# Branch outputs kept as parts, own PSUM tiles, sums on one engine, moved modulation blocks: a change to a two-layer diffusion backbone

## The chip, the core and the metric

One core of a Trainium2 chip runs the whole program. The metric is device time in microseconds (us) from launch to end, the median over executions; lower is better. Engines: TensorE (PE, with its weight loads as PEld), VectorE (DVE), ScalarE (ACT), GpSimd (POOL) and SyncE (SP). DMAs are issued here mostly by SP (loads) and by ACT (stores to scratch in DRAM).

## The reference

Two layers over 512 latent tokens and 256 context tokens of width 1024. Both layers read the context; only the first has to produce it, so layer 0 works on 768 tokens and layer 1 on 512. All is fp32.

```
sh1, sc1, g1, sh2, sc2, g2 = split(silu(c) @ w_mod[l] + b_mod[l], 6)   # per stream
h = adaLN(x, sh1, sc1)
f, nq, nk, nv, cq, ckv, kr, g = split(h @ w_in)
y_f   = real(fft2(f))                     # branch A, 4 channel groups
y_na  = neighbourhood attention(nq, nk, nv) + context keys    # branch B
y_mla = latent attention(cq, ckv, kr)     # branch C
gate  = sigmoid(g)                        # 3 x 1024 per token
mix   = sum_b(gate_b * (y_b @ w_branch_b)) @ w_out
x = LayerNorm(alpha * x + (1 + g1) * mix)
h = adaLN(x, sh2, sc2)
x = LayerNorm(alpha * x + (1 + g2) * ((silu(h @ w_gate) * (h @ w_up)) @ w_down))
```

The modulation vectors (sh1 ... g2) are 12 blocks of 512 columns per layer: blocks 0 and 1 are sh1, 2 and 3 sc1, 4 and 5 g1, 6 and 7 sh2, 8 and 9 sc2, 10 and 11 g2.

## The kernel before, in words

**Precision.** Every large fp32 product is made of three fp32r products: each operand x is kept as a high part (a rounded copy, made by ACT) and a low part (x minus the high part, made by DVE or POOL), and hi x hi, lo x hi and hi x lo are added in PSUM. Activations stand in the big tiles AH and AL; weights are cut the same way as they arrive (whi by ACT at L210, wlo by DVE or POOL at L211).

**Stages of a layer.** Fourier (branch A); NA (branch B, one step per head pair and block of queries); MLA (branch C); gates, whose results are stored in DRAM (gbuf); merge; the out-projection with its LayerNorm (`out_norm`); FFN; the FFN's own out-projection.

**Order.** A step is a Python closure; a list of steps is emitted in program order, and the tile framework then orders each engine's instructions by a timing model of its own. Where steps are `pinned`, PE's order is that of the list. `weave` spreads a list of fill steps between main steps by their costs. PSUM has 8 banks, each held by one tile of `self.ps()`; a bank is written again only after its readers are done. A tile with `bufs` n rotates over n buffers: the next writer of a buffer waits for the last reader, a store included.

**The branch outputs.** Each branch ends in fp32 tiles `ys` (128 channels x tokens), four per branch and layer, which ACT's queue stores to `ybuf[b]` in DRAM (L993 Fourier, L1237 NA, L1543 MLA). In the merge, `y_load(b)` reads branch b back: four times a load from SP into `yr`, a cast to `yh` by ACT (L1630) and a difference `yl` by DVE (L1631).

**The merge.** 24 units (b, j): branch b times output chunk j of 128 channels. `proj` does 4 x 3 matmuls per token range against `w_br` (L1680), then DVE forms (gate + 1) x product from the gate tile `th` and PSUM (L1683) and adds it to `m[j]` (L1686; POOL for branch 1, DVE for branch 2). `th_load` brings the gate tiles two units ahead. `y_load(1)` and `y_load(2)` are issued after unit j = 3 of the branch before; `y_load(0)` in the gates. From unit 4 on, the residual xr is scaled by halves beside it (L1736, POOL, and L1728 for its vectors, DVE). After all units, `split` makes AH and AL of m (ACT L1706, DVE L1707).

**Gates and FFN in seven products.** Gates and FFN work two output chunks at a time by a seven-product scheme (`seven`, matmuls L509). It needs sums and differences of the halves of the activations: `sums` forms whole tiles t = AH + AL (`whole`, L434), differences (`less`, L438), and parts tp of them (`parts`: ACT cast L443, difference L444). There are four such places, the gates and the FFN of each layer. `whole` is done four times and `parts` three times per place, each over 4 chunks; two of the former and two of the latter are on POOL, the rest on DVE.

**The FFN's start.** The hidden chunks 0 and 1 (layer 1: and 2) are done directly, by `unit(f, part)`: g multiplies with `w_gate` and passes SiLU by ACT to `hx` (L1922), u multiplies with `w_up` and DVE multiplies both (L1935). `early` are the units on the first half of the tokens, which run between the transposes (`t0`, `t1`) of the last token blocks out of the LayerNorm; `late` those on the second half. In layer 0, `unit(1, full)` runs over all 768 tokens beside the sums: its context range uses one PSUM tile for both g and u (`s["c", f]`, 2 x 256 columns).

**Modulation blocks.** `mod_fill` makes for each block a step with 32 matmuls (L532) from four 512 KB tiles `mraw` of w_mod, and a finishing step: transposes (L554) and a reduction, or for the gate blocks 4, 5, 10 and 11 one product per half (L544) and a store. Layer 0's first four blocks are done at the start. Its others and layer 1's blocks in MOD_NA are fill in layer 0's NA (12 blocks); layer 1's remaining eight are fill in layer 0's gates.

## Time and profile before

| | |
|---|---|
| median of 3 runs | 2390.05 us (2388.05 to 2396.88) |
| profiled execution, its span | 2387.02 us, 2385.2 us |
| mean granted PE clock | 0.982 |
| busy PE, DVE, ACT, POOL | 95%, 56%, 46%, 42% |
| HBM read, written | 262.06 MB, 47.48 MB |

A line of the profile is named by its line number in the kernel (L1631) and by its tiles, out<-in. Instructions in one row may be several of a kind in a row (x4), the time is then that of all. "[5.56 <-DVE yl L1631]" behind an instruction says that its engine stood idle for 5.56 us before it, and what ended that. The granted clock is PE's, 1.00 being full speed.

### The profile page before, as it was taken

What the parts mean: (1) busy time and instruction counts of PE and PEld (TensorE: products, weight loads), DVE (VectorE), ACT (ScalarE), POOL (GpSimd) and SP (SyncE); (2) the same over time, 40 slices, a digit from 0 to 9 for tenths busy, and PEclk for the clock granted to TensorE, in tenths of its full rate; (3) what the DMA queues carried; (4) which work ended last, traced back from release to release, by engine and by line L of the source; (5) the groups of instructions that cost most, each with busy time, mean ns of one, the idle gap of its engine ahead of it and who ended that gap; (6) DMA issues with size and microseconds to landing.
All of it is one profiled execution on the core that took longest, in us unless ns stands there. A gap on an engine that the chain in (4) does not pass through costs nothing. (4 is left out here: it accounts for less than half of the span.)

```text
span 2385.2 us, 36359 instructions
## 1 busy us (share of the span) xinstructions
PE 2272.1 (95%) x13794; PEld 1971.4 (83%) x13794; DVE 1331.3 (56%) x2339; ACT 1101.7 (46%) x2432; POOL 992.4 (42%) x755
## 2 busy tenths in 40 slices
PE   6999999999999998999999999999999998999997
PEld 4877678878987878999988888787878877999875
DVE  7334456667544568555541462344668458788634
ACT  4335567644432254444442352575765425545532
POOL 2411143124248356334449353324413676323483
PEclk9999999999999999999999999999999999999998
DMA  9436521117674331222262243222214643323432
GB/s 340 145 138 235 187 78 62 54 56 281 225 252 158 115 120 58 98 98 97 71 227 75 80 149 105 79 69 91 87 68 168 207 150 107 113 94 105 142 115 62
DMA packets 105403, 307.71 MB, mean 129 GB/s; under 512 B 12070, under 2 KB 21228, under 8 KB 105228
## 3 DMA queue, kind: packets, MB, share of 16 engines
q1 hardware_dynamic: 86444, 261.48, 32.4%
q10 hardware_dynamic: 15552, 38.63, 4.2%
q0 software_dynamic: 3232, 5.28, 0.8%
q8 instruction: 108, 1.77, 0.3%
q14 instruction: 67, 0.55, 0.1%
HBM read 262.06 MB, written 47.48 MB: 130 GB/s over the span
## 5 line engine op out<-in xcount | busy, mean ns | idle before, releaser
L211 POOL TENSOR_TENSOR wlo<-raw,whi 128x512 fp32r<-128x512 f32 (+2 forms) x420 | 564.4, 1352 | 879.5 <-ACT whi L210 841.6
L210 ACT CAST whi<-raw 128x512 fp32r<-128x512 f32 (+1 forms) x447 | 273.2, 616 | 426.8 <-PE ps L1680 85.7
L509 PE MATMUL ps<-tp,whi 128*128 128x384 f32 (+1 forms) x1120 | 276.0, 316 | 4.9 <-ACT p L481 3.0
L509 PEld LDWEIGHTS ps<-tp,whi 128*128 128x128 f32 x1120 | 196.1, 189 | 9.5 <-ACT p L481 3.4
L509 PE MATMUL ps<-AH,whi 128*128 128x384 f32 (+1 forms) x636 | 199.3, 316 | 4.2 <-DVE hx L490 1.9
L509 PE MATMUL ps<-AH,wlo 128*128 128x384 f32 (+1 forms) x636 | 198.6, 313 | 1.2 <-DVE wlo L211 1.2
L277 PE MATMUL ps<-AH,whi 128*128 128x512 f32 (+1 forms) x584 | 188.4, 367 | 9.8 <-ACT hx L1922 7.4
L509 PE MATMUL ps<-AL,whi 128*128 128x384 f32 (+1 forms) x636 | 197.2, 312 | 0.0
L277 PE MATMUL ps<-AL,whi 128*128 128x512 f32 (+1 forms) x584 | 183.0, 360 | 1.5 <-DVE AL L733 1.5
L277 PE MATMUL ps<-AH,wlo 128*128 128x512 f32 (+1 forms) x584 | 183.5, 360 | 0.0
L509 PE MATMUL ps<-tp,wlo 128*128 128x384 f32 (+1 forms) x560 | 176.4, 315 | 0.4 <-DVE wlo L211 0.4
L2035 PE MATMUL ps<-whi,hx 128*128 128x512 f32 x520 | 164.5, 397 | 8.3 <-ACT hx L2027 4.9
L325 PE MATMUL ps<-whi,AH 128*128 128x512 f32 (+1 forms) x352 | 132.7, 385 | 2.9 <-DVE th L1683 2.9
L325 PE MATMUL ps<-whi,AL 128*128 128x512 f32 (+1 forms) x352 | 134.9, 384 | 0.0
L325 PE MATMUL ps<-wlo,AH 128*128 128x512 f32 (+1 forms) x352 | 134.4, 382 | 0.0
L277 PEld LDWEIGHTS ps<-AH,whi 128*128 128x128 f32 x584 | 101.7, 193 | 34.1 <-ACT hx L1922 7.8
L509 PEld LDWEIGHTS ps<-AH,whi 128*128 128x128 f32 x636 | 120.2, 189 | 7.4 <-DVE hx L490 2.6
L2035 PEld LDWEIGHTS ps<-whi,hx 128*128 128x128 f32 x520 | 99.3, 191 | 31.2 <-ACT hx L2027 5.5
L509 PEld LDWEIGHTS ps<-AH,wlo 128*128 128x128 f32 x636 | 120.3, 189 | 1.8 <-DVE wlo L211 1.6
L509 PEld LDWEIGHTS ps<-AL,whi 128*128 128x128 f32 x636 | 120.0, 189 | 0.8 <-issue 0.8
L277 PEld LDWEIGHTS ps<-AL,whi 128*128 128x128 f32 x584 | 100.0, 191 | 19.7 <-DVE AL L733 2.4
L1736 POOL TENSOR_TENSOR xr<-xr,gb 128x512 f32<-128x512 f32 x80 | 114.5, 1447 | 0.4
(340 smaller groups left out, 5671.1 us busy)
## 6 DMA issues: line engine op xcount, KB each, us to landing
mraw<-in_w_mod_dram SPq DMA_DIRECT2D x80, 512.0 KB
raw<-in_w_down_dram SPq DMA_DIRECT2D x44, 512.0 KB
raw<-in_w_g_dram SPq DMA_DIRECT2D x40, 512.0 KB
raw<-in_w_gate_dram SPq DMA_DIRECT2D x36, 512.0 KB
raw<-in_w_up_dram SPq DMA_DIRECT2D x26, 512.0 KB
raw<-in_w_br_dram SPq DMA_DIRECT2D x24, 512.0 KB
gb<-th ACTq DMA_DIRECT2D x24, 384.0 KB
th<-gb SPq DMA_DIRECT2D x24, 384.0 KB
```

The source lines that it names most:

```text
L210: hi_eng(hi[:, :n], x)
L211: lo_eng.tensor_sub(lo[:, :n], x, hi[:, :n].bitcast(F32))
L277: self.nc.tensor.matmul(ps, w.at(wt, ws), at[:, k0 + kc, cols], start=kc == 0 and i == 0, stop=kc == nk - 1 and i == 2)
L325: self.nc.tensor.matmul(ps, a[:, k0 + kc, tok], w.at(b, ws), start=kc == 0 and i == 0, stop=kc == 2 * nb - 1 and i == 2)
L509: nc.tensor.matmul(ps, ws[0].at(wt, w), act[at], start=new and kc == 0 and i == 0, stop=kc == 3 and i == 2, skip_group_check=True)
L1736: i = op(x[:, c], x[:, c], self.gbt[g][:, c])
L2035: nc.tensor.matmul(ps, h[a][:, tok], w.at(b, ws), start=f == seq[0] and i == 0, stop=f == NF - 1 and i == 2)
```

## The change

Six edits:

- `y_store` replaces the store of a branch output. ACT casts the high part into a tile of its own, DVE subtracts it in place, and ACT's queue stores both parts into two DRAM buffers per branch. Fourier uses one new tile `yh`, NA one of half the tokens, twice per head pair, MLA the tile `qrh` of its queries. `y_load` then is eight loads, no cast and no difference, into four buffers for each part, in two pools in turn; it is issued at the units k = 1 and k = 9.
- g and u of `unit` take a PSUM tile for each range, the context too.
- `sums` has `whole` and `parts` on DVE alone.
- Layer 1's blocks 10 and 11 leave layer 0's NA and go between the early FFN units of layer 1; its blocks 8 and 9 leave layer 0's gates and go between the early FFN units of layer 0. Their first four tiles are loaded right ahead of `out_norm`.
- The split of m into AH and AL is emitted per chunk, in the units of branch 2.
- Some tiles of NA in layer 1 have 512 columns instead of 768.

```diff
@@ -48,7 +48,8 @@
 PB = 1
 PB = 1
 LO_POOL = ((0, 3, 5), (3,))
-MOD_NA = (4, 5, 10, 11)
+MOD_NA = (4, 5)
+MOD_FFN = ((8, 9), (10, 11))
 THP = 2
 MADD_POOL = (True, False)
 PIPE_C = 8
@@ -446,16 +447,16 @@
         def first(ws):
             x, y, z = (self.t("tt", [P, 4, half], f"t{i}") for i in range(3))
             whole(y, 0, e, nc.vector)
-            whole(x, 0, d, nc.gpsimd)
-            whole(z, 4, d, nc.gpsimd)
+            whole(x, 0, d, nc.vector)
+            whole(z, 4, d, nc.vector)
             less(y, x, y)
             less(x, z, x)
             less(z, z, y)
             parts(2, z, nc.vector)
-            parts(3, x, nc.gpsimd)
+            parts(3, x, nc.vector)
             whole(x, 4, e, nc.vector)
             less(x, x, z)
-            parts(4, x, nc.gpsimd)
+            parts(4, x, nc.vector)
             s["t1"] = y
 
         def second(ws):
@@ -602,7 +603,7 @@
         self.A = lambda: (self.AH, self.AL)
         self.mod = [cp.tile([P, 48, 2], F32, name=f"mod{l}") for l in range(DEPTH)]
         self.gvec = [[self.dr.tile([2, D], F32, name=f"gvec{l}{w}") for w in range(2)] for l in range(DEPTH)]
-        self.ybuf = [self.dr.tile([512, T], F32, name=f"yb{b}") for b in range(3)]
+        self.ybuf = [[self.dr.tile([512, T], F32, name=f"yb{b}{i}") for i in range(2)] for b in range(3)]
         self.zbuf = [self.dr.tile([NT, P, D], F32, name=f"zb{l}") for l in range(DEPTH)]
         self.bias = [self.dr.tile([P, H, 2, 256], F32, name=f"bd{l}") for l in range(DEPTH)]
         self.vt1 = cp.tile([P, NV1], F32, name="vt1")
@@ -790,6 +791,19 @@
 
         return [fn(ty, h) for h in range(0, H, BH) for ty in range(2)]
 
+    def y_store(self, b, c, ys, hi, tt, n=1):
+
+
+        nc = self.nc
+        rows = slice(c * P, (c + 1) * P)
+        for i in range(n):
+            cols = slice(i * tt // n, (i + 1) * tt // n)
+            h = hi()[:, :tt // n]
+            nc.scalar.copy(h, ys[:, cols])
+            nc.vector.tensor_sub(ys[:, cols].bitcast(F32R), ys[:, cols], h.bitcast(F32))
+            nc.scalar.dma_start(self.ybuf[b][0][rows, cols], h.bitcast(F32))
+        nc.scalar.dma_start(self.ybuf[b][1][rows, :tt], ys[:, :tt])
+
 
     def fourier_open(self, l):
 
@@ -990,7 +1004,7 @@
                         nc.vector.tensor_add(ys[:, 640:768], rev1(pa), rev1(bs))
                     if s == (1 if cx else 0):
                         tt = T if cx else NLAT
-                        nc.scalar.dma_start(self.ybuf[0][g * P:(g + 1) * P, :tt], ys[:, :tt])
+                        self.y_store(0, g, ys, lambda: self.t("fz", [P, T], "yh", F32R, 1), tt)
                 return f
             return [Step(fn(s), [], (2.7, 0.7)[s]) for s in range(2 if cx else 1)]
 
@@ -1061,7 +1075,7 @@
         halves = [(slice(0, 64), slice(64, 128)), (slice(64, 128), slice(0, 64))]
 
         def ev_q(parts):
-            qs = [self.t(pool, [P, T], f"qs{j}", F32R) for j in range(2)]
+            qs = [self.t(pool, [P, T if cx else NLAT], f"qs{j}", F32R) for j in range(2)]
             for j in range(2):
                 h0, h1 = halves[j]
                 for ps, cols in parts:
@@ -1158,7 +1172,7 @@
                 for j in range(2):
                     nc.gpsimd.tensor_add(bt[:, j], bt[:, j], self.mask)
                 self.bt = bt
-                self.nys = self.t("na", [P, T], "ys", F32, 1)
+                self.nys = self.t("na", [P, tt], "ys", F32, 1)
             kh, kl = self.kk[hp]
             st["ys"], st["p"] = self.nys, []
             if i % 2 == 0:
@@ -1234,7 +1248,7 @@
                                          tile_position=(0, 64 * j), skip_group_check=True)
             nc.vector.tensor_mul(st["ys"][:, (i - 1) * P:(i + 1) * P], y[:, :2 * P], sh["w"])
             if i == (NT if cx else NTL) - 1:
-                nc.scalar.dma_start(self.ybuf[1][hp * P:(hp + 1) * P, :tt], st["ys"][:, :tt])
+                self.y_store(1, hp, st["ys"], lambda: self.t("na", [P, T // 2], "yh", F32R, 1), tt, 2)
 
         f = 1.0 if lat else 0.5
         return dict(scores=scores, norm=norm, transpose=transpose, values=values, c=(0.9 * f, 0.9 * f, 2.0 * f * u))
@@ -1540,7 +1554,7 @@
                                      tile_position=(0, 64 * j))
             nc.vector.tensor_mul(st["ys"][:, (i - 1) * P:(i + 1) * P], y[:, :2 * P], sh["w"])
             if i == nq - 1:
-                nc.scalar.dma_start(self.ybuf[2][hp * P:(hp + 1) * P, :tt], st["ys"][:, :tt])
+                self.y_store(2, hp, st["ys"], lambda: self.t("m3", [P, T], "qrh", F32, 1).bitcast(F32R), tt)
 
         f = 1.0 if lat else 0.33
         return dict(scores=scores, norm=norm, transpose=transpose, values=values, c=(1.95 * f, 1.3 * f, 2.9 * f * u))
@@ -1613,7 +1627,7 @@
         s = {"y": {}}
         fill = []
         if l == 0:
-            fill = self.mod_fill([(1, nb) for nb in range(12) if nb not in MOD_NA], 5)
+            fill = self.mod_fill([(1, nb) for nb in range(12) if nb not in MOD_NA + MOD_FFN[0] + MOD_FFN[1]], 5)
             st += self.bias_steps(1)
         left = 3 * KC - self.ahead[l]
 
@@ -1621,14 +1635,10 @@
             def fn(ws):
                 yh, yl = [], []
                 for c in range(4):
-                    r = self.t("my", [P, tt], "yr", F32, 2)
-                    nc.sync.dma_start(r, self.ybuf[b][c * P:(c + 1) * P, :tt])
-                    i = (4 * b + c) % 7
-                    pool, n = ("my", 4) if i < 4 else ("mg", 3)
-                    yh.append(self.t(pool, [P, tt], "yh", F32R, n))
-                    yl.append(self.t(pool, [P, tt], "yl", F32R, n))
-                    nc.scalar.copy(yh[c], r)
-                    nc.vector.tensor_sub(yl[c], r, yh[c].bitcast(F32))
+                    pool = ("my", "mg")[b % 2]
+                    for i, (x, tag) in enumerate(((yh, "yh"), (yl, "yl"))):
+                        x.append(self.t(pool, [P, tt], tag, F32R, 4))
+                        nc.sync.dma_start(x[c].bitcast(F32), self.ybuf[b][i][c * P:(c + 1) * P, :tt])
                 s["y"][b] = (yh, yl)
             return Step(fn)
 
@@ -1684,6 +1694,10 @@
                                                    ALU.add, ALU.mult)
                 if b > 0:
                     (nc.gpsimd if MADD_POOL[b - 1] else nc.vector).tensor_add(m, m, th)
+                if b == 2:
+                    nc.scalar.activation(self.AH[:, j, :tt], m, AF.Copy, scale=0.5)
+                    nc.vector.scalar_tensor_tensor(self.AL[:, j, :tt], m, 0.5, self.AH[:, j, :tt].bitcast(F32),
+                                                   ALU.mult, ALU.subtract)
             return [Step(fn, [(io["w_br"][l, b, j // 2], 1024, "w")] if j % 2 == 0 else [], 3.9 if cx else 2.6)]
 
 
@@ -1693,7 +1707,7 @@
             if k + 2 < len(units):
                 main += [th_load(k + 2)]
             main += proj(b, j)
-            if j == 3 and b < 2:
+            if k in (1, KC + 1):
                 main += [y_load(b + 1)]
             if k == 0:
                 main += [self.open("xr", "left"), self.open("gb", "left"), Step(lambda ws: self.load_xr(l, nt))]
@@ -1701,14 +1715,10 @@
                 main += [Step(lambda ws, i=k - SCALE_AT: self.scale_xr(i // 2, True, (i % 2,)))]
         st += [Step(m_open)] + main
 
-        def split(ws):
-            for j in range(KC):
-                nc.scalar.activation(self.AH[:, j, :tt], s["m"][j], AF.Copy, scale=0.5)
-                nc.vector.scalar_tensor_tensor(self.AL[:, j, :tt], s["m"][j], 0.5,
-                                               self.AH[:, j, :tt].bitcast(F32), ALU.mult, ALU.subtract)
-
-        st += [Step(split), self.close("gb", "mg", "my")]
-        st += [self.open("ln", "left"), Step(lambda ws: self.ln_open(l, 0, cx))]
+        st += [self.close("gb", "mg", "my")]
+        st += [self.open("ln", "left"), Step(lambda ws: self.ln_open(l, 0, cx)), self.open("mod", "left")]
+        begin, *self.mods = self.mod_fill([(1, nb) for nb in MOD_FFN[l]], 4)
+        st += [begin]
         self.out_norm(l, 0, [[(io["w_out"][l, nh, b], 1024, "w") for b in range(4)] for nh in range(2)], self.A, None, 3)
 
     def load_xr(self, l, nt):
@@ -1909,12 +1919,8 @@
                 if ws:
                     s["g", f] = ws[0]
                 pr = []
-                s["c", f] = self.ps() if CTX in part else None
                 for c in part:
-                    if c == CTX:
-                        pr.append((s["c", f][:, :NCTX], c))
-                    else:
-                        pr.append((self.ps()[:, :c.stop - c.start], c))
+                    pr.append((self.ps()[:, :c.stop - c.start], c))
                 block(s["g", f], pr)
                 if ("sg", f) not in s:
                     s["sg", f] = self.t("fx", [P, tt], "hx", F32, 4)
@@ -1926,10 +1932,7 @@
                     s["u", f] = ws[0]
                 pr = []
                 for c in part:
-                    if c == CTX:
-                        pr.append((s["c", f][:, NCTX:], c))
-                    else:
-                        pr.append((self.ps()[:, :c.stop - c.start], c))
+                    pr.append((self.ps()[:, :c.stop - c.start], c))
                 block(s["u", f], pr)
                 for ps, cols in pr:
                     nc.vector.tensor_mul(h_tile(f)[:, cols], s["sg", f][:, cols], ps)
@@ -1979,8 +1982,9 @@
         late = [Step(unit(f, [d])[k], [], c) for f, k in parts]
         t0, t1 = self.tail_tr
         tp, t_sums, t_first = self.sums(tt // 2)
-        st += pinned(early[:1] + [t0] + early[1:2] + [t1] + early[2:] + late)
-        st += [self.close("ln", "xr"), self.open("ft", "right"), self.open("tt", "right"), t_sums]
+        m0, m1 = self.mods[:2], self.mods[2:]
+        st += pinned(m0[:1] + early[:1] + [t0] + m0[1:] + early[1:2] + [t1] + m1[:1] + early[2:] + m1[1:] + late)
+        st += [self.close("mod", "ln", "xr"), self.open("ft", "right"), self.open("tt", "right"), t_sums]
         g, u = unit(1, full)
         rg, ru = reqs(1)
         if cx:
```

## Rows read from the trace of the kernel before

**Rows 1.** The page's first part: busy us of each engine, share of the span, instructions.

```profile
PE 2272.1 (95%) x13794; PEld 1971.4 (83%) x13794; DVE 1331.3 (56%) x2339; ACT 1101.7 (46%) x2432; POOL 992.4 (42%) x755
```

**Rows 2.** Waits of PE: line, what released it; us in total, times, longest.

```profile
PE ps L277 <- ACT hx L1922: 7.4, 1, 7.4
...
PE ps L1680 <- DVE yl L1631: 5.6, 1, 5.6
...
PE ps L1680 <- DVE m L1683: 3.1, 1, 3.1
```

**Rows 3.** Windows around gaps: us, busy (PE, PEld, DVE, ACT, POOL), PEclk, DMA share, GB/s.

```profile
703.50:710.53 7.03, 3.89 (x23) 3.11 (x22) 6.48 (x6) 2.44 (x4) 6.52 (x4) 1.00 0.86 328
710.53:714.10 3.57, 3.57 (x9) 2.88 (x10) 3.57 (x8) 0.83 (x1) 3.57 (x4) 0.52 0.83 251
...
772.66:778.90 6.24, 6.24 (x19) 5.38 (x20) 4.60 (x6) 1.46 (x2) 5.29 (x3) 0.51 0.26 84
879.40:890.72 11.32, 7.10 (x46) 6.51 (x45) 10.21 (x20) 7.61 (x17) 7.92 (x6) 1.00 0.56 189
890.72:894.95 4.23, 4.23 (x15) 4.23 (x16) 4.23 (x4) 0.47 (x1) 4.13 (x3) 0.60 0.00 0
...
922.37:925.70 3.33, 3.33 (x16) 3.33 (x17) 0.51 (x2) 1.28 (x3) 3.33 (x3) 0.51 0.00 0
...
1988.56:2007.85 19.29, 13.26 (x106) 12.45 (x105) 18.04 (x31) 11.56 (x26) 15.07 (x8) 1.00 0.39 136
2021.84:2035.57 13.73, 8.47 (x48) 6.58 (x46) 13.26 (x27) 8.92 (x20) 10.18 (x6) 0.85 0.35 116
2035.57:2038.40 2.83, 2.83 (x13) 2.83 (x14) 0.97 (x2) 0.00 (x0) 2.35 (x2) 0.51 0.51 178
```

**Rows 4.** Timeline of ACT, FFN of layer 0: start, us, instruction, idle before.

```profile
921.04 0.51 ACT L443 CAST tp<-t 128x384 fp32r<-128x384 f32 x1 [1.63 <-DVE t L438]
```

**Rows 5.** Timeline of DVE, then of POOL, in the merge of layer 0.

```profile
705.90 3.98 DVE L1631 TENSOR_TENSOR yl<-yr,yh 128x768 fp32r<-128x768 f32 x2
...
760.59 12.02 DVE L1631 TENSOR_TENSOR yl<-yr,yh 128x768 fp32r<-128x768 f32 x1 [0.62 <-ACT yh L1630]
...
777.17 1.05 DVE L1707 SCALAR_TENSOR_TENSOR AL<-m,AH 128x768 fp32r<-128x768 f32 x1 [0.91 <-ACT AH L1706]
...
766.33 1.81 POOL L1686 TENSOR_TENSOR m<-m,th 128x768 f32<-128x768 f32 x1
768.10 2.48 POOL L1736 TENSOR_TENSOR xr<-xr,gb 128x512 f32<-128x512 f32 x2
```

**Rows 6.** Instructions by line: ns min/median/max, first and last start us.

```profile
L1631 DVE TENSOR_TENSOR yl<-yr,yh x24: 678/973/12018, 558.3 to 1914.0; 128x768 fp32r<-128x768 f32 x12, 128x512 fp32r<-128x512 f32 x12
...
L1630 ACT CAST yh<-yr x24: 614/725/847, 550.6 to 1913.3; 128x768 fp32r<-128x768 f32 x12, 128x512 fp32r<-128x512 f32 x12
...
L444 POOL TENSOR_TENSOR tp<-t,tp x32: 740/1310/5956, 536.7 to 2035.5; 128x384 fp32r<-128x384 f32 x16, 128x256 fp32r<-128x256 f32 x16
L444 DVE TENSOR_TENSOR tp<-t,tp x16: 411/549/1379, 535.1 to 2026.4; 128x384 fp32r<-128x384 f32 x8, 128x256 fp32r<-128x256 f32 x8
```

**Rows 7.** Timeline of POOL, FFN of layer 1.

```profile
2026.63 10.06 POOL L444 TENSOR_TENSOR tp<-t,tp 128x256 fp32r<-128x256 f32 x4 [2.75 <-ACT tp L443]
```

**Rows 8.** Timeline of PE: one mod block, its two finishes.

```profile
171.17 1.02 PE L544 MATMUL ps<-modsb,sel 128*2 128x512 f32 x2
...
677.36 1.93 PE L532 MATMUL ps<-mraw,sT 128*32 128x256 f32 x32
...
687.76 0.60 PE L554 MATMUL ps<-ident,modsb 128*128 128x128 f32 x4
```

**Rows 9.** Window over branch B (NA) of layer 0, columns as in rows 3.

```profile
150.00:347.00 197.00, 191.64 (x1454) 146.22 (x1453) 93.16 (x257) 106.22 (x328) 45.48 (x39) 0.98 0.47 164
```

**Rows 10.** Timeline of ACT, then of DVE, in the gates of layer 1.

```profile
1863.78 0.33 ACTq L1592 DMA_DIRECT2D gb<-th  x1
...
1868.45 0.42 DVE L487 TENSOR_TENSOR th<-ps,p 128x256 f32<-128x256 f32 x1 [4.89 <-DMA gb<-th]
```

## The prediction

> **What bounds the kernel now.** I read the page first: TensorE (PE) is busy 2272.1 of 2385.2 us, 95%, and no other engine passes 56% [rows 1]. The kernel is matmul-bound, so time is won only where PE stands still, and where it runs slowly afterwards: the clock row of the page (not needed here) is full nearly everywhere, so the places to look for are single gaps. The list of PE's waits names them: 7.4 us once for the SiLU tile hx of the FFN's first blocks, 5.6 us once for yl, the low part of a branch output, 3.1 us once for the first gated sum m [rows 2]. Then I cut windows around each gap, to see the idle time and the granted clock behind it. After every one of these gaps the clock stands at 0.51 to 0.60 of full, the lower of its two levels (1.2 against 2.4 GHz), for 3.3 to 6.2 us [rows 3]. So a gap costs its length and, behind it, the stretch at half clock times (1 minus the clock). Both are in my sum; the second part is where PE is "busy" and yet loses.
>
> **The change part by part.** Gains are negative, in us of the profiled execution.
>
> *A, own PSUM tiles for gate and up of the first FFN blocks (layer 0).* Before, the context columns of gate and up share one PSUM bank, so up's context matmuls wait until ScalarE (ACT) has read gate's. That read, hx, is queued on ACT behind the casts of the sums, each of which waits for VectorE (DVE): the cast just ahead of it started at 921.04 after 1.63 us of waiting [rows 4]. PE waited 7.4 us [rows 2], then ran 3.33 us at clock 0.51 [rows 3]: 7.4 + 3.33 x 0.49 = 9.0. With its own bank up needs nothing of hx. Behind it come products that need the sums' parts, which may not be ready. If they were ready no sooner than hx was, only the context block itself would be won: 24 matmuls, of which 16 took 3.33 us at 0.51, so 24 x 3.33 / 16 x 0.51 = 2.5. Ends -2.5 and -9.0; I take **-8.0**, since the sums' parts are spread over that stretch and only a last one should be late.
>
> *B, the split of branch outputs leaves the merge: branch 2 in layer 0.* One DVE difference (L1631) took 12.02 us, against a median of 0.97 for this line, while GpSimd (POOL) ran back to back beside it [rows 5, 6]. PE stood 5.6 us [rows 2] and then ran 6.24 us at 0.51: 5.6 + 6.24 x 0.49 = 8.7. After the change these parts come from DRAM ready-made; the line is gone. What could be late next is another DVE instruction with two SBUF inputs that falls into the same crowded stretch: the split of m (L1707), which the change emits here chunk by chunk; but the scheduler had put it at 777.17, right behind, already [rows 5], so the per-chunk edit by itself I cost at 0. Ends 0 and -8.7, I take **-8.0**.
>
> *C, the same at the merge's start in layer 0.* DVE finishes scaling at about 705.9, then does two such differences, 3.98 us, and only then the sum m that PE waits for [rows 5]. The wait is 3.1 us [rows 2], the clock costs 3.57 x 0.48 = 1.7: 4.8. But the DMA engines are 0.86 busy there at 328 GB/s [rows 3], and the change reads each branch output as two parts: 8 loads of 384 KB instead of 4, for branch 1 issued at unit 1 where PE stands here. I leave 1.4 to the DMA and take **-3.4** (ends 0 and -4.8).
>
> *D, sums on VectorE alone.* At each of the four places 16 two-input operations (8 sums L434, 8 differences L444) move from POOL to DVE. POOL's L444 has a median of 1.31 us and a longest of 5.96, DVE's 0.55 [rows 6]; DVE gets 16 x 0.55 = 8.8 us more work per place. In the FFN of layer 1 PE is busy 8.47 of 13.73 us, 5.3 idle, while POOL takes 10.06 us for four L444 [rows 3, 7]; the clock at 0.85 over that window and 0.51 behind it costs 13.73 x 0.15 + 2.83 x 0.49 = 3.4, of which the first part also counts idle time, so some 2.6: 7.9 in all. DVE is 13.26 of 13.73 busy there, so its 16 operations at the shortest 0.41 [rows 6] add up to 6.6 us of DVE time against POOL's 10.06: part of the wait stays. I take **-6.0** (ends +3 and -7.9). The other three places have no such gap on PE: 0.
>
> *E, mod blocks moved into the FFN's starts.* A block is 32 matmuls, 1.93 us, and a finish of 0.60 (transposes, blocks 8 and 9) or 1.02 (blocks 10 and 11) [rows 8]. The four come to 2 x (1.93 + 0.60) + 2 x (1.93 + 1.02) = 10.96 us of PE, taken out of the attention of layer 0, where PE is busy 191.64 of 197 [rows 9], and out of a gate stretch without idle time: there they are nearly all gain. They go between the first FFN blocks, where PE idles 11.32 - 7.10 = 4.2 us (layer 0) and 19.29 - 13.26 = 6.0 (layer 1), with 4.23 x 0.40 = 1.7 of clock behind the first [rows 3]: 11.9 us of room for 10.96 of work. Their order is pinned, so not every block meets a hole; those that miss move without gain. The 2 MB of mod weights are issued on SP (SyncE's queue) ahead of w_out's loads, where DMA has room. I take **-7.0**, ends 0 and -11.0.
>
> *F, the split at the branches.* What the merge loses, 12 casts and 12 differences per layer (0.73 and 0.97 us at the median) [rows 6], the branches gain, on engines half idle there (ACT 106.22 of 197, DVE 93.16) [rows 9]. New is a wait: the tile of the high part is single (one in the Fourier stage, one of half width in NA, a borrowed query tile in MLA), so the next copy into it waits on ACT until the store has landed. The trace of before has no such store, the nearest is the gates' tile: stored by ACT at 1863.78, and DVE could write it again at 1868.45 after 4.89 us of idling [rows 10], some 4.7 us from issue. Behind the waiting copy, ACT's exponentials and casts of the next head pair are queued, and PE waits for those. In NA the two halves follow each other directly, 8 stores a run; in MLA 8 more. Ends: 0 (the scheduler puts other ACT work between, or PE has enough ahead) and 16 x 4.7 = 75. I take **+4**, near the lower end, because ACT has half its time free and the instruction order is planned around a wait that the planner knows of.
>
> Smaller tiles for layer 1 cost and give nothing that these rows show: 0.
>
> Sum: -8.0 - 8.0 - 3.4 - 6.0 - 7.0 + 4 = -28.4. The profiled execution took 2387.0 (its span is 2385.2); 2387.0 - 28.4 = 2358.6. It lay 3.0 under the median of the runs, 2390.05, so the forecast is 2361.6.
>
> **The rivals.**
> *R1, slower: ACT is held at the stores.* For: ACT runs in order, two copies in NA meet the same half tile at once, and landing took 4.7 us [rows 10]. Against: ACT half idle, PE's waits in NA are 5.4 us in 197 now [rows 9]. Price: at 3 us of PE for each of 16 stores, 48 in place of 4: 2406. It decides from 2.0 us a store on: (2390 - 2357.6) / 16.
> *R2, the merge becomes a matter of DMA.* Each branch now brings 3.1 MB in one burst, 9 us at 328 GB/s, in stretches already 0.86 full [rows 3]; gates' and weights' loads stand behind it on SP. B and C (11.4) are lost and half of E: 2361.6 + 11.4 + 3.5 = 2376.5. Against: the burst is issued seven units, over 25 us, before its use.
> *R3, DVE and POOL slow each other.* The 12.02 us beside a busy POOL [rows 5] shows that a DVE difference can take twelve times its length, and POOL still has its weight splits. Then the sums, now all on DVE, are no faster: D's 6.0 and 5.5 of A go, and the sums of the two out-projections' gates lose 1.5 each: 2361.6 + 14.5 = 2376. The Trainium skill ("GPSIMD Engine Reference", section "1. Specifications") says that GpSimd shares its SBUF interfaces with VectorE, in contention with DVE instructions with two SBUF inputs, and these sums are such; the 12.02 us row agrees with it. By that rule the other way out is also open: less POOL work is less contention, which is my -6.0.
> *R4, the gaps move.* The order on each engine is planned anew for the whole kernel; new gaps of the old size elsewhere give 2388. For: the gaps of before stand although a planner laid out the order. Against: A and B are single, named causes, which are removed.
>
> **How the numbers follow.** Forecast 0.52 (by itself 2350 to 2371), R1 0.13, R2 0.10, R3 0.12, R4 0.13. What a measurement can tell from no change is 0.5%, 12 us: faster is below 2378, slower above 2402. Faster: 0.52 and three quarters of R2 and R3, 0.17, together 0.69. Slower: R1 without its milder part, 0.11. The rest, 0.20, is the same. The upper ends together, 9.0 + 8.7 + 4.8 + 7.9 + 11.0 = 41.4 with F at 0, give 2349; I set the low end at 2346, and the high end at 2392, past R4, so that R1 is what is left out.
>
> **What the changed profile would show.** A: no wait of PE for hx, ctx matmuls of up directly behind the latent ones. B, C: L1631 gone, no half clock in branch 2 of layer 0's merge; the y loads finished before unit 8 and 16. D: four L444 of layer 1's FFN in a row on DVE at 0.4 us. E: mod matmuls between the transposes of the FFN's start, fewer idle us there, and attention of layer 0 shorter by 5 to 6. F: ACT idle ahead of the copies in y_store, released by DMA; if these idle times exceed 2 us and PE's waits in NA and MLA grow with them, it is R1 and I am wrong. I am also wrong if PE's idle total hardly falls while all the named gaps are gone.

## The result and the profile after

The changed kernel took 2367.48 us (median of 4 runs, 2355.63 to 2371.37) against 2389.05 us for the kernel before (4 runs): a ratio of 0.9904, 95% interval 0.9886 to 0.9921. It is faster by about 1%, 21.6 us; 28.4 were forecast. Its profiled execution took 2369.68 us.

The page's first part and the main waits of PE in the changed kernel (line numbers are higher by 1 to 15 after the edits; columns as in [rows 1, 2]):

```profile
PE 2264.3 (96%) x13794; PEld 1965.7 (83%) x13794; DVE 1292.1 (55%) x2411; ACT 1106.2 (47%) x2440; POOL 934.1 (39%) x691
```

```profile
PE ps L326 <- ACT AH L1698: 6.9, 1, 6.9
PE ps L278 <- POOL wlo L212: 5.1, 1, 5.1
...
PE ps L510 <- ACT p L482: 4.2, 4, 2.4
...
PE ps L533 <- DMA mraw<-in_w_mod_dram: 2.7, 1, 2.7
```

The three named waits of [rows 2] are gone (hx, yl, m), but others stand here: for the split of m (AH) at the end of layer 1's merge, for a weight difference (wlo) on POOL in layer 1's FFN start, for mod weights in layer 0's gates, and for copies p. The last are not new in sum (4.5 us in four waits before), but 3.4 of the 4.2 us are now in layer 0's FFN, where there were none. PE works the same 13794 matmuls in 7.8 us less than in [rows 1], at a mean granted clock of 0.985 for 0.982, and idles 9.5 us less (2385.2 - 2272.1 = 113.1 before, 2367.9 - 2264.3 = 103.6 after), where the three waits alone were 16.1. One more thing is odd at first sight: DVE does 72 more instructions in 39 us less. Some 14 us of that come with the sums alone (1317.3 us busy in that kernel, below); the merges do 33 us less (65.80 to 41.01 and 37.39 to 29.44 below), and part of that is done in the branches now.

Windows over the two merges, changed kernel, layer 0 and layer 1 (columns as in [rows 3]):

```profile
683.20:788.00 104.80, 104.80 (x602) 92.46 (x602) 41.01 (x64) 22.84 (x34) 86.15 (x58) 1.00 0.70 253
1846.60:1924.80 78.20, 71.31 (x319) 58.99 (x318) 29.44 (x34) 19.20 (x33) 61.45 (x49) 0.96 0.72 253
```

and the same stretches in the kernel before:

```profile
688.10:805.20 117.10, 108.40 (x592) 94.16 (x591) 65.80 (x77) 28.82 (x42) 81.64 (x57) 0.96 0.58 199
1868.80:1942.90 74.10, 71.20 (x319) 58.90 (x318) 37.39 (x44) 24.48 (x43) 68.68 (x49) 0.98 0.64 209
```

Layer 0's merge has no idle PE left and is 12.3 us shorter; layer 1's is 4.1 longer, with 6.9 us of idle PE. That idle time stands in its last part, where the DMA share is 0.24:

```profile
1890.00:1915.00 25.00, 18.11 (x79) 14.67 (x78) 12.03 (x6) 4.38 (x7) 23.05 (x19) 0.92 0.24 75
```

In the 40 us ahead of it, shown below under the spread loads, the share is 0.95 and PE is never idle.

To see where time went, I cut each trace at the first matmul of a stage, or at the last of the one before. The table gives the lengths before, and the difference for the changed kernel and for four kernels that have one part of it each. They are single executions, so differences under about 2 us say nothing alone.

| stage (layer) | before, us | changed | parts | PSUM | sums | mods |
|---|---|---|---|---|---|---|
| start | 158.2 | +1.2 | -0.2 | -0.3 | +1.5 | +0.6 |
| NA (0) | 195.7 | -7.4 | -0.9 | -0.8 | -1.1 | -8.0 |
| MLA (0) | 179.6 | +1.3 | +1.3 | +0.1 | -0.5 | +1.2 |
| gates (0) | 154.6 | 0.0 | +2.0 | +0.1 | +1.4 | -3.9 |
| merge (0) | 117.1 | -12.3 | -13.1 | -8.3 | +0.5 | -1.6 |
| out_norm, FFN start (0) | 95.7 | +1.3 | +1.7 | 0.0 | -1.5 | +1.3 |
| FFN (0) | 318.4 | -3.6 | +1.3 | +4.7 | -5.5 | +1.1 |
| down (0), Fourier (1) | 300.4 | 0.0 | -0.1 | -0.1 | -1.7 | +0.2 |
| NA, MLA (1) | 282.3 | +0.2 | +2.3 | +0.3 | -1.8 | +0.4 |
| gates (1) | 66.8 | -2.9 | +0.5 | -0.2 | -2.3 | -0.1 |
| merge (1) | 74.1 | +4.1 | +5.1 | +0.1 | +0.2 | -4.1 |
| out_norm, FFN start (1) | 71.6 | +2.1 | +0.3 | +1.5 | +0.5 | +8.5 |
| FFN, down (1) | 353.7 | -1.8 | -1.0 | -1.3 | -8.2 | +1.3 |
| sum | 2368.2 | -17.8 | -0.8 | -4.2 | -18.5 | -3.1 |

The PSUM kernel's profiled execution was its second fastest of 12 (2382.86, median 2392.57), so its column flatters it; that of the mods kernel was its slowest (2383.89, median 2381.91).

One entry teaches more than the rest: the PSUM kernel gains 8.3 us in layer 0's merge, which its edit doesn't touch. The wait for yl isn't there. The DVE difference that took 12.02 us in [rows 5] stands at the same place, beside the same kinds of POOL operations, but is short:

```profile
759.46 1.34 DVE L1631 TENSOR_TENSOR yl<-yr,yh 128x768 fp32r<-128x768 f32 x1 [0.62 <-ACT yh L1630]
```

In the other kernels that keep this difference it took 12.05 to 12.37 us. So the long hold can be absent in a kernel that does the same work here, and a gain of 8 us in this merge doesn't need stored parts.

### The profile page after: what moved, and what is told of

Its sections match the earlier page's. It is cut to its first block, busy times and chain, and to the rows that moved or that the text cites. A ratio compares the mean times of both kernels' runs of the same rounds, so it can differ in the third digit from the quotient of the medians.

```text
span 2367.9 us, 36388 instructions
## 1 busy us (share of the span) xinstructions
PE 2264.3 (96%) x13794; PEld 1965.7 (83%) x13794; DVE 1292.1 (55%) x2411; ACT 1106.2 (47%) x2440; POOL 934.1 (39%) x691
## 5 line engine op out<-in xcount | busy, mean ns | idle before, releaser
L212 POOL TENSOR_TENSOR wlo<-raw,whi 128x512 fp32r<-128x512 f32 (+2 forms) x420 | 588.1, 1410 | 928.2 <-ACT whi L211 876.9
L510 PEld LDWEIGHTS ps<-AH,wlo 128*128 128x128 f32 x636 | 120.5, 189 | 1.0 <-POOL wlo L212 0.6
L278 PEld LDWEIGHTS ps<-AH,wlo 128*128 128x128 f32 x584 | 100.3, 193 | 21.5 <-POOL wlo L212 5.4
```

The source lines that it names most:

```text
L212: lo_eng.tensor_sub(lo[:, :n], x, hi[:, :n].bitcast(F32))
L278: self.nc.tensor.matmul(ps, w.at(wt, ws), at[:, k0 + kc, cols], start=kc == 0 and i == 0, stop=kc == nk - 1 and i == 2)
L510: nc.tensor.matmul(ps, ws[0].at(wt, w), act[at], start=new and kc == 0 and i == 0, stop=kc == 3 and i == 2, skip_group_check=True)
```

## The experiments

Four kernels: before, with one part of the change each.

**Stored parts alone.** `y_store` and `y_load` (with its new places k = 1 and 9), and the smaller tiles.

```diff
-                nc.scalar.dma_start(self.ybuf[1][hp * P:(hp + 1) * P, :tt], st["ys"][:, :tt])
+                self.y_store(1, hp, st["ys"], lambda: self.t("na", [P, T // 2], "yh", F32R, 1), tt, 2)
...
-                    yh.append(self.t(pool, [P, tt], "yh", F32R, n))
+                        nc.sync.dma_start(x[c].bitcast(F32), self.ybuf[b][i][c * P:(c + 1) * P, :tt])
```

> The kernel before with y_store and y_load alone. My theory: it carries the whole gain in layer 0's merge, both waits (yl, m) and the half clock behind them gone, that merge 12 us shorter, and costs 1 to 3 us in NA and MLA: 8 to 11 us faster than before. Rival R1 (ACT held at the stores): NA and MLA together more than 10 us longer, no gain. On the new wait of PE for mod weights at the start of layer 0's gates (2.7 us idle, 3.4 us of clock in the changed kernel): if the eight y loads ahead of them on SP cause it, it is here; if a slow weight split on POOL beside the sums causes it, it is not here. On the 6.9 us wait for AH at the end of layer 1's merge: if the split of m per chunk causes it, it is not here; if the new loads do, it is.

Measured: ratio 0.9995 (0.9983 to 1.0008), 2387.78 us: nothing. Layer 0's merge is 13.1 us shorter, and all of it is paid back elsewhere. Hardly by ACT: the copies of `y_store` in the changed kernel waited for DVE only, never for a store.

```profile
L802 ACT CAST yh<-ys x24: 389/512/837, 81.3 to 1631.8; 128x384 fp32r<-128x384 f32 x8, 128x256 fp32r<-128x256 f32 x8, 128x768 fp32r<-128x768 f32 x4, 128x512 fp32r<-128x512 f32 x4
...
L802 ACT CAST qrh<-ys x8: 622/740/855, 418.9 to 1783.2; 128x768 fp32r<-128x768 f32 x4, 128x512 fp32r<-128x512 f32 x4
...
  DVE ys L998: 10.9, 4
  DVE ys L1249: 8.0, 3
  DVE ys L1555: 4.9, 2
  DVE ys L1004: 2.9, 4
```

(The lines below the two are what ended ACT's idle time ahead of them: four kinds, all DVE.) One other copy did wait for a store: MLA's own cast into the borrowed tile qrh, twice, 1.8 us in all (1.8 with stored parts alone too). The longer of the two, with the store issued ahead of it:

```profile
1712.59 0.33 ACTq L804 DMA_DIRECT2D yb<-qrh  x1
...
1714.65 0.61 ACT L1449 CAST qrh<-qr 32x512 fp32r<-32x512 f32 x1 [1.60 <-DMA yb<-qrh]
```

The hold on DVE is not gone from layer 0's merge either. In the stretch where the branch's difference took 12 us, the addition to m now takes as long, here with stored parts alone:

```profile
765.69 11.04 DVE L1695 TENSOR_TENSOR m<-m,th 128x768 f32<-128x768 f32 x1
```

Without the sums it is 10.59 us, in the changed kernel nothing is held there. But PE is busy for all of this merge in each of these kernels (104.00 of 104.00 us here), so this addition, unlike yl, had time to spare. The edit took away the instruction for which PE waited, and not the hold.

NA and MLA are 2.7 us longer in both layers together (-0.9, +1.3 and +2.3), within the 1 to 3 that were expected and far from R1's 10. So R1 is out. The largest payback is layer 1's merge, +5.1, where PE waits 5.3 us for AH; the split per chunk is not in this kernel, so it is not needed for that wait. No wait for mod weights is here, so the eight loads alone do not make it.

**Own PSUM tiles alone.**

```diff
-                s["c", f] = self.ps() if CTX in part else None
                 for c in part:
-                    if c == CTX:
-                        pr.append((s["c", f][:, :NCTX], c))
-                    else:
-                        pr.append((self.ps()[:, :c.stop - c.start], c))
+                    pr.append((self.ps()[:, :c.stop - c.start], c))
```

> The kernel before with own PSUM tiles for g and u alone. The step A of the prediction: the 7.4 us wait for hx goes and only a late part of the sums remains, 8 us faster. My theory now, from the changed kernel, where 1.1 and 2.4 us of waits for p copies stand in its place: about half of it comes back, 3 to 5 us faster, because ACT's queue is still full of casts that wait for VectorE. Rival: nothing is won, the same wait moves behind the context block, within 1 us of before.

Measured: ratio 1.0016 (0.9999 to 1.0032): no gain, if anything a loss. The wait for hx is gone, but PE runs into the same chain a little later (timeline of PE in layer 0's FFN; in brackets the idle time and what ended it):

```profile
913.68 0.44 PE L509 MATMUL ps<-AH,whi 128*128 128x384 f32 x1 [1.06 <-ACT whi L210]
916.77 0.45 PE L509 MATMUL ps<-AH,wlo 128*128 128x384 f32 x1 [2.65 <-POOL wlo L211]
925.45 0.69 PE L509 MATMUL ps<-tp,whi 128*128 128x384 f32 x1 [6.12 <-ACT p L481]
```

9.8 us in three waits, for the 7.4 that were there. The bank held PE up, but the products behind it were not ready either.

**Sums on VectorE alone.**

```diff
-            whole(x, 0, d, nc.gpsimd)
-            whole(z, 4, d, nc.gpsimd)
+            whole(x, 0, d, nc.vector)
+            whole(z, 4, d, nc.vector)
...
-            parts(3, x, nc.gpsimd)
+            parts(3, x, nc.vector)
...
-            parts(4, x, nc.gpsimd)
+            parts(4, x, nc.vector)
```

> The kernel before with the sums on VectorE alone. Step D of the prediction: layer 1's FFN start 6 us shorter and nothing else moves, 6 us faster. My theory now: VectorE's unbroken row of two-input sums holds POOL off, so a weight split on POOL takes over 5 us and PE waits for it in layer 1's FFN start, about as long as it waited for POOL's differences before: within 3 us of before, with a POOL wlo of over 5 us in the trace (before at most 2.6). The wait for mod weights in layer 0's gates is here if it comes from a slowed split on POOL.

Measured: ratio 0.9916 (0.9899 to 0.9933), 2368.27 us: 20 us faster, nearly the whole gain of the change, from the edit that was expected to give 0 to 6. My theory of a gain given back fell here: no POOL difference took over 4.96 us, and layer 1's FFN is 6.4 us shorter. One part of the reason can be read from a window, layer 0's sums, before (first row) and with sums on VectorE (second fence):

```profile
895.90:923.10 27.20, 19.82 (x104) 17.37 (x104) 26.84 (x32) 9.82 (x20) 20.66 (x14) 0.92 0.10 34
```

```profile
895.90:923.10 27.20, 26.95 (x154) 24.37 (x153) 25.91 (x48) 11.14 (x22) 9.32 (x4) 1.00 0.10 35
```

DVE was full in both. Before, it finished 32 instructions in 26.84 us, beside POOL at work for 20.66 us; with POOL's share given to it, it finished 48 in 25.91 us. The same 64 DVE differences of the sums, which both kernels have, show the speed like for like (busy us, mean ns of one), before and with sums on VectorE:

```profile
L438 DVE TENSOR_TENSOR t<-t,t 128x384 f32<-128x384 f32 x32 | 26.6, 860 | 0.1
L438 DVE TENSOR_TENSOR t<-t,t 128x256 f32<-128x256 f32 x32 | 20.8, 680 | 2.0 <-POOL t L434 2.0
```

```profile
L438 DVE TENSOR_TENSOR t<-t,t 128x384 f32<-128x384 f32 x32 | 16.0, 544 | 0.0
L438 DVE TENSOR_TENSOR t<-t,t 128x256 f32<-128x256 f32 x32 | 11.7, 410 | 0.0
```

860 ns became 544, and 680 became 410. So DVE took over POOL's share at hardly any cost: its sums take 94.1 us in all with the 64 more, for 90.2 before. The last part is ready at about the time it was before, 1.2, 0.3 and 1.6 us earlier and 1.0 later, counted from the first sum of each place.

PE is busy 26.95 of 27.20 us in place of 19.82. The wait for hx (7.4 us in [rows 2]) is gone in this kernel although gate and up still share their bank. Here the speed is one part and the order that the planner laid out anew is the other. ACT's copy hx came behind ten casts of the sums before (the eighth of them, then hx):

```profile
917.02 0.51 ACT L443 CAST tp<-t 128x384 fp32r<-128x384 f32 x1 [0.56 <-DVE t L438]
...
921.46 0.86 ACT L1922 ACTIVATE hx<-ps 128x512 f32<-128x512 f32 x2
```

and behind eight with sums on VectorE:

```profile
913.95 0.51 ACT L443 CAST tp<-t 128x384 fp32r<-128x384 f32 x1 [0.89 <-DVE t L438]
914.36 0.87 ACT L1922 ACTIVATE hx<-ps 128x512 f32<-128x512 f32 x2
```

The eighth cast is 3.1 us earlier, hx 7.1: some 3 us are the faster sums, some 4 the two casts fewer. The kernel with stored parts alone, whose sums are as before but whose planner also put hx behind eight casts, waits 3.2 us for hx in place of 7.4. In layer 1's FFN the order of PE's products changed too, and its eighth part is ready 12.8 us after the stage's start for 12.4 before, so the gain there can't be read as an earlier sum. No run kept the order of before with the sums moved, so how much of the 20 us is speed and how much order is open.

**Mod blocks alone.** MOD_FFN, the fill in `begin` and the pinned order as in the change.

```diff
-        st += pinned(early[:1] + [t0] + early[1:2] + [t1] + early[2:] + late)
+        m0, m1 = self.mods[:2], self.mods[2:]
+        st += pinned(m0[:1] + early[:1] + [t0] + m0[1:] + early[1:2] + [t1] + m1[:1] + early[2:] + m1[1:] + late)
```

> The kernel before with the four mod blocks moved alone. Step E of the prediction: 7 us faster (ends 0 and 11). My theory now: NA of layer 0 is 6 to 7 us shorter, layer 0's gates 5 us shorter (no wait for mod weights there, since no y loads stand before them), and the FFN starts get 1 to 2 us longer each: 8 to 10 us faster. Rival: the blocks do not meet the holes of the FFN starts, these get 5 us longer each, within 2 us of before. If the 5.1 us wait for wlo in layer 1's FFN start is here, it comes from the mod blocks and not from the sums.

Measured: ratio 0.9968 (0.9957 to 0.9980), 7.6 us by 0.0032 x 2388, near the 7.0 of step E, but in part by luck. NA -8.0 and gates -3.9, against +1.3 in layer 0's FFN start, where the blocks met the holes, and +8.5 in layer 1's, where they did not (5.9 us of work, 2.6 on top). Another 4.1 us came off in layer 1's merge, where nothing was forecast.

**The change without the sums.** The sums of before in the changed kernel.

> The changed kernel with the sums on GpSimd and VectorE as before, so the other five edits without this one. My theory, from the parts alone (stored parts 0, own PSUM tiles +4, mod blocks -7): 2383 to 2389, within 5 us of before. Rival: with all of them together the gaps of the merge and of the FFN are gone, 2372 or less.

Measured: ratio 0.9976 (0.9964 to 0.9988), 2383.18 us. The other five edits together are worth 0.24%; with the sums it is 0.96%. In layer 0's FFN PE waits 5.9 us for p, though gate and up have tiles of their own here, as it did with own tiles alone (6.1). On top of the sums the same five bring 0.12% (0.9904 against 0.9916), with intervals that overlap.

**Sums and mod blocks together.** Both diffs above on the kernel before.

> The kernel before with the sums on VectorE and the mod blocks moved, without stored parts, own PSUM tiles and the split per chunk. My theory: what was measured alone adds up, 20 and 7 us: 2361 to 2363, faster than the changed kernel by 4 to 6. Rival: the wait for wlo in layer 1's FFN start (5.1 us and 3.4 of clock in the changed kernel) comes from these two together, and the time is 2366 to 2370, the changed kernel's. The rival to both, that stored parts carry a gain once the sums are on VectorE: 2372 or more.

Measured: ratio 0.9922 (0.9910 to 0.9934), 2367.75 us. They do not add up: with the sums there, the mod blocks bring nothing that shows beyond 0.9916. PE waits 5.1 us for a weight difference on POOL here as in the changed kernel, and runs behind it at a granted clock of 0.52 for 3.5 us, the lower level. Most of what the sums won in layer 1's FFN is missing again (-2.3 for -8.2), and its start is 7.5 us longer, for 5.9 us of work in the mod blocks. In the changed kernel that place looks so (timelines of DVE, then POOL, then POOL's whole line with shortest, median and longest in ns):

```profile
1993.88 4.10 DVE L435 TENSOR_TENSOR t<-AH,AL 128x256 f32<-128x256 f32 x12
1997.91 1.41 DVE L439 TENSOR_TENSOR t<-t,t 128x256 f32<-128x256 f32 x4
1999.25 0.40 DVE L1938 TENSOR_TENSOR hst<-hx,ps 128x256 f32<-128x256 f32 x1
...
2002.13 0.67 DVE L212 TENSOR_TENSOR wlo<-ss,whi 128x512 fp32r<-128x512 f32 x1
```

```profile
1994.49 10.67 POOL L212 TENSOR_TENSOR wlo<-raw,whi 128x512 fp32r<-128x512 f32 x2 [4.86 <-issue]
```

```profile
L212 POOL TENSOR_TENSOR wlo<-raw,whi x420: 993/1294/9440, 25.6 to 2334.9; 128x512 fp32r<-128x512 f32 x127, 128x416 fp32r<-128x416 f32 x10, 128x384 fp32r<-128x384 f32 x3
```

DVE's row runs on at 0.34 us a sum, and one POOL difference takes 9.44 us for 1.29. In the merge it is the other way round: one addition on DVE, 9.26 us for 0.69 elsewhere, beside POOL's row, which holds back AH and PE (the 6.9 us above). It also began late, since the product ahead of it waited 9.50 us for its gate tile, whose load was issued on SP only at 1900.74 (DVE, SP, then POOL):

```profile
1903.62 0.69 DVE L1693 SCALAR_TENSOR_TENSOR th<-th,ps 128x512 f32<-128x512 f32 x1 [9.50 <-DMA th<-gb]
1904.34 9.26 DVE L1696 TENSOR_TENSOR m<-m,th 128x512 f32<-128x512 f32 x1
```

```profile
1900.74 2.82 SPq L1670 DMA_DIRECT2D th<-gb  x2
```

```profile
1904.41 1.29 POOL L212 TENSOR_TENSOR wlo<-raw,whi 128x512 fp32r<-128x512 f32 x1
1905.66 1.28 POOL L1746 TENSOR_TENSOR xr<-xr,gb 128x512 f32<-128x512 f32 x1
1906.90 1.27 POOL L1696 TENSOR_TENSOR m<-m,th 128x512 f32<-128x512 f32 x1
1908.13 4.92 POOL L212 TENSOR_TENSOR wlo<-raw,whi 128x512 fp32r<-128x512 f32 x4
```

The same addition was held in the other kernels with stored parts too: 8.25 us with stored parts alone, 9.40 without the sums.

**That difference moved to VectorE.** For the one block, in the changed kernel and in the kernel with sums and mod blocks.

```diff
-                                          nc.gpsimd) for c in range(0, k, size)], size)
+                                          nc.vector if pool == "dve" else nc.gpsimd) for c in range(0, k, size)], size)
...
+        su = Step(u, ru, 7.8, 4)
+        if not cx:
+            su.pool = "dve"
```

> The changed kernel with one edit: the two weight differences of layer 1's one direct FFN block (w_up of chunk 1) on VectorE instead of GpSimd. My theory: the 5.1 us wait for wlo and the 3.4 us of clock behind it are POOL's difference held off by VectorE's sums; on VectorE it takes its turn, the wait goes, 5 to 8 us faster than the changed kernel, 2360 to 2364. Rival: VectorE is full there, the wait stays as one for VectorE's wlo or for later parts of the sums, within 2 us of the changed kernel.

> The same edit on the kernel with sums and mod blocks alone, where the same wait stands. My theory: 2360 to 2363, the two parts then add up. Rival: 2366 to 2369, as without the edit.

Measured: 0.9885 (0.9870 to 0.9900), 2361.41 us, in the first, and 0.9931 (0.9919 to 0.9944), 2370.26 us, in the second. The wait is gone in both. In the second nothing is won: PE's waits of over 0.25 us, added up from the FFN's first direct product to its first down product, fall only from 10.2 us in 10 waits to 8.4 in 14, most of them now short ones for DVE. The first is the fastest kernel measured, but its interval overlaps the changed kernel's (0.9886 to 0.9921), and the two were not timed in one series: faster than before by 1.15%, faster than the change not shown.

**Loads spread.** The changed kernel, two loads of a branch output per unit over four units.

```diff
-            if k in (1, KC + 1):
-                main += [y_load(b + 1)]
+            if b < 2 and 1 <= j <= 4:
+                main += [y_load(b + 1, (j - 1,))]
```

> The changed kernel with the eight loads of a branch output in the merge issued two per unit over four units instead of all in one. My theory: layer 1's merge lost 4 to 5 us because the burst holds the gates' loads back and VectorE and GpSimd then have their work bunched; spread, that merge is 74 us again and the kernel 3 to 5 us faster than the changed one. Rival: it is the amount, not the burst, and nothing changes, within 2 us.

Measured: 0.9926 (0.9914 to 0.9938), 2368.52 us, no gain; layer 1's merge is 77.1 us, the wait for AH still 5.8. So the burst is not needed for the longer merge; the amount may be. The middle of that merge in the changed kernel:

```profile
1850.00:1890.00 40.00, 40.00 (x189) 33.58 (x188) 10.28 (x16) 9.82 (x17) 33.78 (x28) 1.00 0.95 342
```

and in the kernel before:

```profile
1872.00:1912.00 40.00, 40.00 (x188) 33.57 (x187) 17.87 (x23) 13.90 (x24) 37.86 (x29) 1.00 0.73 238
```

342 GB/s for 238, and PE busy throughout in both; POOL, which needs the loaded weights, gets 4 us less done here and has them to do at the end, in the row beside which DVE's addition was held. That the amount alone does it wasn't tried.

**The change without own PSUM tiles.**

> The changed kernel without the own PSUM tiles (gate and up share one for the context again). Step A of the prediction: 8 us slower than the changed kernel, the wait for hx back. My theory: hx was late because of the casts behind slowed sums, so with the sums on VectorE the shared tile costs nothing: within 2 us of the changed kernel, no wait for hx over 1 us.

Measured: 0.9933 (0.9919 to 0.9947), 2369.82 us, 2.3 above the changed kernel's median. That one is from another series; by the ratios the distance is 0.29%, some 7 us, and the intervals just overlap. In the traces layer 0's FFN is 1.6 us longer without the tiles, and the wait for hx is 0.7 us. Between nothing and a few us, what the tiles are worth beside the sums isn't settled.

**The two engines side by side, by themselves.** Two kernels of elementwise rows: in the first the framework had mixed the phases and successive results shared a tile, so the rows have pauses; in the second each result has its own tile and the order is fixed.

> Nothing of the reference is computed: rows of elementwise operations on VectorE and GpSimd are laid beside each other, in seven phases. My theory: whichever of the two engines runs an unbroken row of two-input operations on SBUF keeps the other out until its row pauses. Phase 1 (24 DVE additions of two SBUF tiles, one POOL difference): POOL's one takes about 9 us, the whole row, instead of 1.3. Phase 2 (DVE's second input in PSUM): 1.3. Phase 3 (DVE copies, one SBUF input): not known, 1.3 or 9. Phase 4 (each sixth DVE addition from PSUM): POOL gets in at such a place, 2 to 4 us. Phase 5 (one DVE addition beside 8 POOL differences): DVE's takes about 10 us instead of 0.7. Phase 6 (the same with PSUM): 0.7. Rival: the two share fairly and each takes about double, 2.6 us for POOL in phase 1 and 1.4 for DVE in phase 5.

> Nothing of the reference is computed: six phases of elementwise operations, each result in a tile of its own and the order on VectorE and GpSimd fixed, so that the rows have no pauses. My theory: the engine whose unbroken row of two-input SBUF operations came first keeps the other out until it pauses. Phase 1 (24 DVE additions, 8 us; one POOL difference of 128x256 begins just behind their start): POOL's takes 7 to 9 us. Phase 2 (second input in PSUM): under 1 us. Phase 3 (copies, one SBUF input): not known, under 1 or 6 to 8. Phase 4 (each sixth addition from PSUM): POOL gets in at the first such place, 1.5 to 3 us. Phase 5 (8 POOL differences of 128x512, 10 us, one DVE addition begins behind the first): DVE's takes 9 to 11 us. Phase 6 (the same with PSUM): 0.4. Rival: one for one, as rows with pauses in them did: POOL's takes under 2 us in phase 1 and DVE's under 2 in phase 5.

The first (DVE, then POOL):

```profile
30.00 0.41 DVE L44 TENSOR_TENSOR e<-a,b 128x256 f32<-128x256 f32 x1
...
30.93 8.81 DVE L44 TENSOR_TENSOR e<-a,b 128x256 f32<-128x256 f32 x7
```

```profile
32.43 11.13 POOL L38 TENSOR_TENSOR k<-a,b 128x512 f32<-128x512 f32 x8
```

Seven additions, of which one alone takes 0.41 us (the first row), took 8.81 us, 1.26 each: one DVE instruction for each of POOL's. The second, DVE's single addition behind the first instruction of a POOL row, with its second input in SBUF and then in PSUM, and POOL's rows beside them:

```profile
40.77 1.47 DVE L73 TENSOR_TENSOR q<-f,b 128x256 f32<-128x256 f32 x1 [0.83 <-POOL f L68]
...
51.97 0.42 DVE L75 TENSOR_TENSOR q<-f,ps 128x256 f32<-128x256 f32 x1 [0.83 <-POOL f L68]
```

```profile
7.41 0.84 POOL L60 TENSOR_TENSOR g<-d,b 128x256 f32<-128x256 f32 x1 [0.54 <-DVE d L59]
16.52 0.72 POOL L60 TENSOR_TENSOR g<-d,b 128x256 f32<-128x256 f32 x1 [8.27 <-DVE d L59]
...
40.69 9.98 POOL L71 TENSOR_TENSOR z<-a,b 128x512 f32<-128x512 f32 x8
...
51.89 9.80 POOL L71 TENSOR_TENSOR z<-a,b 128x512 f32<-128x512 f32 x8
```

With two SBUF inputs the addition takes 1.47 us and ends 0.3 us behind the POOL instruction it ran into (1.25 us of the row, from 40.69); with one input in PSUM 0.42, as if POOL were not there. POOL's difference beside 24 unbroken DVE additions took 0.84 against 0.72 beside additions with an input in PSUM (the first two POOL rows). These are single executions. The rival held, one for one, and my theory that an unbroken row keeps the other out for its whole length fell for such rows: they show no hold of 9 us.

## Why the prediction was right, and where it was wrong

The time lay in the range and on the forecast side, at 2367.5 for 2361.6, but that the sum came out near is luck: its errors cancel. One term was over three times too small, and it carries seven eighths of the gain; the others, 22.4 us by the forecast, measure 3 to 6 together (0.12% on top of the sums, 0.24% without them).

- **B and C** (-11.4): right in place and size, layer 0's merge is 12.3 us shorter, 13.1 with this part alone. It was not the hold that went, but the instruction for which PE had no time to spare: with stored parts alone an addition is held 11.04 us there, and PE never stands still. B's long difference can also be short without the edit, as the PSUM kernel's 1.34 us shows, and the kernel as a whole gains nothing from this part alone (see F).
- **A** (-8.0, PSUM tiles): wrong. Alone the tiles give nothing (1.0016). The step that failed is the choice of an end near -9.0, for which the parts behind the context block had to be ready: they weren't, and PE waited 9.8 us for them. [rows 4] had the sign of it, the cast ahead of hx waiting 1.63 us for DVE. The 7.4 us went by the sums edit without this one, some 3 by faster sums and some 4 by the new order on ACT.
- **D** (-6.0): the place was right, layer 1's FFN is 6.4 us shorter with sums alone, but the term was mis-sized, 20 us in all. I counted what POOL no longer delays and charged DVE 16 x 0.55 us for the work. I left out that POOL's 16 operations had slowed DVE's own, though [rows 6] has DVE's L444 at 0.55 median and 1.38 longest: freed of them, DVE's differences L438 fall from 860 to 544 ns and from 680 to 410, so the charge of 16 x 0.55 us was all but repaid. I also left out the order: the sums end about when they did, and part of the gain, in layer 1's FFN above all, comes with a new order of ACT and PE that no run holds apart. R3 named the contention and priced it with the wrong sign, as the cost of moving sums to DVE, where it was the cost of leaving them on POOL; its last sentence has the right sign, but books it in the -6.0, whose working has no such term. The Trainium skill ("GPSIMD Engine Reference", section "1. Specifications") names DVE instructions with two SBUF inputs as those that contend with GpSimd; 1.47 against 0.42 us agrees.
- **E** (-7.0): near in size alone (-7.6), with luck: layer 1's half missed the holes (+8.5 for 5.9 us of work), and 4.1 us came in a merge that was not in the sum. On top of the sums it no longer shows (0.9922 against 0.9916).
- **F** (+4): the wait it priced is all but absent: 1.8 us of ACT at the borrowed tile, landing some 2 us behind issue for the 4.7 taken, and NA and MLA 2.7 us longer, so R1 did not come. What costs more I left at nothing: the stored parts gain 13.1 us in layer 0's merge and end at 0.9995, with 5.1 of it lost in layer 1's merge and the rest in pieces of up to 2.3 us. R2 had the merges in mind, but layer 0's gain stands at a DMA share of 0.70, and in layer 1's PE is busy where the share is 0.95 and waits where it is 0.24, behind POOL's row and a late gate tile. Whether the loads lie behind that is open.
- **The split of m per chunk** (0): not tried alone. The wait at the end of layer 1's merge stands without it too (5.3 us with stored parts alone).
- **R4**, gaps that move, was right in part: the three waits of [rows 2], 16.1 us together, are gone, and waits of 6.9, 5.1 and 2.7 us stand in the changed kernel that were not there. The prediction's own last sign of being wrong, gaps gone and PE's idle total hardly less, came half true, with 9.5 us less. The wait for mod weights stands in the changed kernel, and without own tiles (2.9 us), but in none of the single parts, nor in sums and mod blocks together, nor in the change without the sums: it seems to take the sums and one of the two edits to the merge.

Open: why single instructions were held for 9.26, 9.44 and 12.02 us in these kernels, when rows of the same operations by themselves go one for one. Each of these three ended 0.5 to 1.2 us after the other engine's row had come to a pause, which fits a row that keeps the other engine out; the rows by themselves, and the 1.34 us in the PSUM kernel, do not. Open too: what lengthens layer 1's merge, and how the gain of the sums divides between speed and order.

## What to carry to other kernels

When two engines share one chain of elementwise work, taking the work from the slower one is not to be priced at the other's free time alone: compare the mean with the shortest duration of the same instruction at one shape, since the difference is a first estimate of what the helper costs. A wait's releaser names the last link only; undo one part at a time before a gain is booked to an edit, and look whether the planner gave another order, since that is a change of its own. A gap closed in one stage can come back in another, here in the merge of the other layer, so add up all stages.

## What the runs showed of the hardware

In rows by themselves, a DVE addition of two SBUF tiles that met a POOL instruction ended 0.3 us behind it (1.47 us for 0.42); with one input in PSUM it took 0.42 beside the same row. Seven such additions beside a POOL row took 1.26 us each, one for each of POOL's. In whole kernels the shares were not always so even: single instructions of either engine were held for 8.25 to 12.37 us beside a busy row of the other, and the one of 12.02 us took 1.34 in another kernel. DVE's differences in the sums took 860 and 680 ns (mean, two shapes) with POOL on the same chain, 544 and 410 without it. A store from ACT's queue released its tile some 2 us after it was issued.
